# The opening of a two-layer trunk kernel: the first chunk's P1 and P2 moved ahead of the pair's eight steps

## The chip, the core and the metric

The kernel runs on one core of one Trainium2 chip. The core has five engines that run side by side and meet at semaphores: TensorE (matmuls; PE in the profile, its weight loads PEld), VectorE (DVE), ScalarE (ACT), GpSimd (POOL) and SyncE (SP, which here only issues transfers). Matmuls write into PSUM, which has eight banks of 128 x 512 fp32; everything else lies in SBUF, in tiles of 128 partitions. The metric is device microseconds of one execution, median of several runs. Each engine works through its own list of instructions in order, and each instruction starts when the tiles that it reads are written and the buffer that it writes is free.

## The reference

A trunk of two layers over 512 positions of width 1024, in fp32. Each layer has a SwiGLU block, a mixer and a second SwiGLU block, each after an RMSNorm, each added to the stream. The first layer's mixer is a gated linear recurrence, the second's a causal spatial gate.

```python
def swiglu(x, w_in, w_out):
    g, u = jnp.split(x @ w_in, 2, axis=-1)
    return (jax.nn.silu(g) * u) @ w_out
...
    for i in range(DEPTH):
        h = h + 0.5 * swiglu(rms_norm(h, ffn1_norm[i]), ffn1_w_in[i], ffn1_w_out[i])
        hn = rms_norm(h, mix_norm[i])
...
        h = h + m
        h = h + 0.5 * swiglu(rms_norm(h, ffn2_norm[i]), ffn2_w_in[i], ffn2_w_out[i])
    return rms_norm(h, final_norm)
```

The change touches only the start of the very first SwiGLU block: x (512 x 1024) times w_in (1024 x 5632), with the norm's gain on x's columns and its root on the result's rows.

## The kernel before

**One product.** An fp32 product is made of three matmuls: each operand is split into a high part, rounded to the format that TensorE reads (ScalarE copies it, `act` in L96), and a low part, the rest (VectorE subtracts, `tt` in L87 for weights, `stt` in L93 for x). The three are high by high, low by high and high by low. For x the blocks are turned by TensorE first (L267, a matmul with the identity), and the split reads the turned block out of PSUM with the norm's gain as its scale.

**Seven products instead of eight.** Large multiplications run through `seven` (L338): both operands are cut in 2 x 2 blocks and multiplied by a Strassen-Winograd scheme. Its seven products are P1 (A11), P2 (A12), P5 (S1), P6 (S2), P3 (S4), P7 (S3) and Q4 (A22), in this order, where A11 to A22 are quarters of the left operand and S1 to S4 sums of them (L46, L47). P1 and P6, P7, Q4 share the accumulators A, P2 has B, P5 and P3 have C (L48); each accumulator is two banks, one for each 128 rows. A stays open from P1 to Q4. Each product takes two steps, for its two halves of the inner dimension.

**Steps.** The program is a list of steps, `subs`. A step has a weight block of 128 x 1024 fp32 (`raw`, eight buffers), which it splits into `whi` and `wlo` (four buffers each), and twelve matmuls of 128 x 512. The main loop (L1457 to L1473) writes the program step by step: what is hooked to the step's phases "pre", "mid", "rest", the splits of the steps up to three ahead (`ahead`, L213, for the first ones), new loads as far as buffers are free (`load_more`), then the step's matmuls, then what is hooked to "end" and "late". So the place of every instruction in its engine's list is fixed here. A split that finds all four buffers taken waits for the matmuls of the step that used the oldest.

**Banks.** Of the eight banks six serve products (`bank`, L74) and two serve transposes and small things (`aux`, L77). A bank that the program asks for is one that an earlier tile has left, and the first matmul into it waits for that tile's last reader.

**The opening.** The first SwiGLU's columns are worked through as a pair (256 columns of gate and of value together, `pair_plain`, L736) and then chunks of four times 128. The pair isn't a `seven`: it multiplies A12, A11 (the first 256 rows: half 0), A22, A21 (the other rows: half 1) by its four weight blocks, each of which serves both halves, so the second half's four steps are `Again` and hold the split buffers of the first four until then. In steps 0 to 7 the pair runs; steps 8 and 9 are the chunk's P1, 10 and 11 P2, 12 and 13 P5, and so on. Because x's inverse root is not known yet, the pair's results wait for it: silu of half 0 in step 7, `post(0)` in step 8 (`stt` out of the banks p into h, L775), `post(1)` in step 9. The chunk's B takes its banks from `aux` here (`spare`).

**Loads.** SP issues loads in the order of the program: x's right half of the first 256 rows in two transfers of 256 columns, the first pair block in four transfers, the second in two, then x's left half, two more pair blocks (two transfers each), the other rows of x, and blocks as buffers come free. A pair block has rows of 1 KB (256 columns), or is cut further; a chunk's block has rows of 2 KB. Some blocks get a second block added by an accumulating transfer that GpSimd issues (`add`, L136), two steps after their load.

**The start of TensorE.** Before x arrives, TensorE runs matmuls on a tile of zeros (`warm_up`, L1381). Then A12's first block is turned, two more warm-ups, A12's second block, two more; the blocks are split together with the first weight blocks (L1423 to L1430). A11 is turned in the middle of step 1, A22 at the end of step 2, A21 at the end of step 3. `value` (L1412) copies a turned block unsplit, for the sums.

## Time and profile before

| | |
|---|---|
| median of 3 runs | 1618.13 us |
| lowest and highest | 1617.69, 1618.21 us |
| the profiled execution's own time | 1618.02 us |
| its span in the profile | 1616.1 us |
| granted TensorE clock | 0.999 |
| read from HBM | 275.84 MB, 172 GB/s over the span |

The profile is of one execution. The page's share of an engine is busy time over the span. Matmuls overlap in the pipeline: a matmul of 128 x 512 is shown with 0.39 us, and the next one starts 0.23 us after it. In a view by time a row merges like instructions of one line: start, time from the first's start to the last's end, engine, line, operation, tiles, count, and in brackets how long the engine was idle before it and what ended that. The page names the tiles by the program's names: `e` is a turned block, `hi` and `lo` its split, `whi` and `wlo` a weight block's, `raw` the block itself, `p`, `A`, `B`, `C` the accumulators, `h` the gated result.

### The profile page before, as it was taken

What the parts mean: (1) busy time and instruction counts of PE and PEld (TensorE: products, weight loads), DVE (VectorE), ACT (ScalarE), POOL (GpSimd) and SP (SyncE); (2) the same over time, 40 slices, a digit from 0 to 9 for tenths busy, and PEclk for the clock granted to TensorE, in tenths of its full rate; (3) what the DMA queues carried; (4) which work ended last, traced back from release to release, by engine and by line L of the source; (5) the groups of instructions that cost most, each with busy time, mean ns of one, the idle gap of its engine ahead of it and who ended that gap; (6) DMA issues with size and microseconds to landing.
All of it is one profiled execution on the core that took longest, in us unless ns stands there. A gap on an engine that the chain in (4) does not pass through costs nothing.

```text
span 1616.1 us, 20846 instructions
## 1 busy us (share of the span) xinstructions
PE 1604.8 (99%) x7451; PEld 1327.6 (82%) x7451; DVE 1373.2 (85%) x1839; ACT 1036.9 (64%) x1504; POOL 223.0 (14%) x201
## 2 busy tenths in 40 slices
PE   9999999999999999999999999999999999999998
PEld 7888888898888888888888888888888788888886
DVE  6898888888998787877987978878978988879778
ACT  7656556668776556656775565566886766565665
POOL 2111111100011111111101111111211011111110
PEclk9999999999999999999999999999999999999999
DMA  8767876844383786866837768768877557686693
GB/s 279 180 171 169 209 181 156 216 124 115 87 213 83 187 215 150 215 164 161 207 88 182 173 171 212 179 155 204 219 189 189 155 125 188 170 207 159 162 206 99
DMA packets 164695, 279.29 MB, mean 173 GB/s; under 512 B 11520, under 2 KB 38000, under 8 KB 164592
## 3 DMA queue, kind: packets, MB, share of 16 engines
q1 hardware_dynamic: 115088, 184.84, 36.4%
q0 software_dynamic: 47712, 91.30, 33.6%
q10 hardware_dynamic: 1792, 1.84, 0.4%
q8 instruction: 58, 0.95, 0.2%
q14 instruction: 45, 0.37, 0.1%
HBM read 275.84 MB, written 2.10 MB: 172 GB/s over the span
## 4 chain that ended last, share of the span: by engine, by line
PE 98%; ACT 1%; DMA 1%; DVE 0%; SPq 0%; issue 0%; DVEq 0%; ACTq 0%
PE A L367 14%; PE A L369 14%; PE A L368 14%; PE C L367 8%; PE C L368 8%; PE C L369 8%; PE p L760 5%; PE B L367 4%; PE B L369 4%; PE B L368 4%; PE e L267 4%; PE r L227 2%; PE r L225 2%; PE r L226 2%; PE Q L367 1%; PE Q L369 1%
## 5 line engine op out<-in xcount | busy, mean ns | idle before, releaser
L96 ACT ACTIVATE whi<-raw 128x1024 fp32r<-128x1024 f32 (+1 forms) x536 | 553.8, 1034 | 379.4 <-PE A L368 100.6
L87 DVE TENSOR_TENSOR wlo<-raw,whi 128x1024 fp32r<-128x1024 f32 (+1 forms) x537 | 638.6, 1191 | 182.2 <-ACT whi L96 180.8
L367 PE MATMUL A<-whi,hi 128*128 128x512 f32 x1016 | 403.9, 397 | 0.0
L369 PE MATMUL A<-wlo,hi 128*128 128x512 f32 x1016 | 396.7, 390 | 0.0
L368 PE MATMUL A<-whi,lo 128*128 128x512 f32 x1016 | 396.3, 390 | 0.0
L369 PEld LDWEIGHTS A<-wlo,hi 128*128 128x128 f32 x1016 | 190.7, 188 | 41.8 <-DVE wlo L87 0.3
L368 PEld LDWEIGHTS A<-whi,lo 128*128 128x128 f32 x1016 | 191.1, 188 | 38.0 <-DVE lo L87 0.6
L367 PEld LDWEIGHTS A<-whi,hi 128*128 128x128 f32 x1016 | 190.9, 188 | 37.4
L367 PE MATMUL C<-whi,hi 128*128 128x512 f32 x560 | 218.4, 390 | 0.0
L368 PE MATMUL C<-whi,lo 128*128 128x512 f32 x560 | 218.0, 389 | 0.0
L369 PE MATMUL C<-wlo,hi 128*128 128x512 f32 x560 | 217.9, 389 | 0.0
L137 POOL DMA_DIRECT2D raw<-in_ffn_w_in_dram x82 | 98.8, 1205 | 742.3 <-DVE raw L87 477.5
L137 POOL DMA_DIRECT2D raw<-in_ffn_w_out_dram x72 | 83.3, 1205 | 373.4 <-DVE wlo L87 158.9
L87 DVE TENSOR_TENSOR raw<-raw,raw 128x1024 f32<-128x1024 f32 x108 | 129.5, 1199 | 1.1 <-DMA raw<-in_ffn_w_out_dram 0.6
L87 DVE TENSOR_TENSOR lo<-a,hi 128x512 fp32r<-128x512 f32 (+1 forms) x188 | 122.2, 658 | 3.8 <-ACT hi L96 3.4
L96 ACT ACTIVATE hi<-a 128x512 fp32r<-128x512 f32 (+1 forms) x188 | 112.5, 601 | 20.2 <-DVE a L87 17.0
L368 PEld LDWEIGHTS C<-whi,lo 128*128 128x128 f32 x560 | 105.1, 188 | 22.1 <-DVE lo L87 0.2
L369 PEld LDWEIGHTS C<-wlo,hi 128*128 128x128 f32 x560 | 105.1, 188 | 21.8
L367 PEld LDWEIGHTS C<-whi,hi 128*128 128x128 f32 x560 | 105.1, 188 | 21.7
L96 ACT ACTIVATE c<-A 128x512 f32<-128x512 f32 x132 | 77.4, 594 | 54.9 <-PE A L369 54.9
L367 PE MATMUL B<-whi,hi 128*128 128x512 f32 x280 | 112.0, 400 | 0.0
L369 PE MATMUL B<-wlo,hi 128*128 128x512 f32 x280 | 109.3, 390 | 0.0
(161 smaller groups left out, 2103.7 us busy)
## 6 DMA issues: line engine op xcount, KB each, us to landing
raw<-in_ffn_w_in_dram SPq DMA_DIRECT2D x162, 512.0 KB, 4.4
raw<-in_ffn_w_out_dram SPq DMA_DIRECT2D x100, 512.0 KB, 5.6
raw<-in_ffn_w_in_dram POOLq DMA_DIRECT2D x82, 512.0 KB, 7.5
raw<-in_ffn_w_out_dram POOLq DMA_DIRECT2D x60, 512.0 KB, 7.6
raw<-in_sg_w_in_dram SPq DMA_DIRECT2D x20, 512.0 KB, 6.3
raw<-in_rec_w_in_dram SPq DMA_DIRECT2D x16, 512.0 KB, 4.0
raw<-in_ffn_w_in_dram SPq DMA_DIRECT2D x30, 256.0 KB, 5.1
raw<-in_sg_w_in_dram POOLq DMA_DIRECT2D x12, 512.0 KB, 8.1
```

Of the source, the lines that this page charges most:

```text
L87: nc.vector.tensor_tensor(out=o, in0=x, in1=y, op=op)
L96: nc.scalar.activation(out=o, in_=x, func=f, **k)
L137: nc.gpsimd.dma_start(out=self.v, in_=src, accum_op=ALU.add)
L225: nc.tensor.matmul(ps, wh, xh, start=start, stop=False)
L226: nc.tensor.matmul(ps, wh, xl, start=False, stop=False)
L227: nc.tensor.matmul(ps, wl, xh, start=False, stop=stop)
L267: nc.tensor.transpose(ps[:, o : o + P], src(q, s), ident)
L367: nc.tensor.matmul(ps, zh, wh, start=fresh and i == 0, stop=False, **k)
L368: nc.tensor.matmul(ps, zl, wh, start=False, stop=False, **k)
L369: nc.tensor.matmul(ps, zh, wl, start=False, stop=end, **k)
L760: nc.tensor.matmul(bank_of(half, s), z, (sub.lo if m == 2 else sub.hi)[:, q, :], start=left[2] == "2" and (h, q, m) == (0, 0, 0), stop=lef ...
```

## The change

P1 and P2 of the first chunk become steps 0 to 3, the pair steps 4 to 11; from step 12 on (P5) the order is as before. Therefore A11 is turned and split first and A12 in the middle of step 1 (`second_blocks`, now on banks of the products), A22 and A21 at the ends of steps 4 and 6 instead of 2 and 3. The first weight block is now the chunk's, loaded in two transfers of 2 KB rows, and x's first half comes in one transfer of 2 KB rows; A11's first block is split by quarters, the high part of the first by VectorE. P1's matmuls alternate between its two banks. The pair's matmuls have one order in all cases. `post(0)` stands in step 11, `post(1)` in step 13, the root in step 8, and the silu of c1 nine steps after P2. B's banks come from `bank`. The warm-ups are 6 and 2 instead of 5, 2 and 2.

```diff
         def fetch(self):
-            nc.sync.dma_start(out=self.v, in_=self.src)
+            for q in ((slice(0, 1), slice(1, 2)) if self.halves else (slice(0, self.shape[1]),)):
+                nc.sync.dma_start(out=self.v[:, q, :], in_=self.src[:, q, :])
...
-        def split(self, vector=False):
+        def split(self, between=None):
...
-                if vector:
-                    nc.vector.tensor_copy(self.hi[:, q, :], src[:, q, :])
-                else:
-                    act(self.hi[:, q, :], src[:, q, :], AF.Copy)
+                act(self.hi[:, q, :], src[:, q, :], AF.Copy)
                 tt(self.lo[:, q, :], src[:, q, :], f32(self.hi[:, q, :]), ALU.subtract)
+                if between is not None and q.start == 0:
+                    between()
...
-    ahead = {0: 1, 1: 1, 2: 3, 3: 3, 4: 3}
+    ahead = {0: 1, 1: 2, 2: 3, 3: 4, 4: 6, 5: 7}
...
-                        bk[name, s] = (spare if name == "B" else bank)(name)[:, :w]
+                        bk[name, s] = bank(name)[:, :w]
...
+                if opening and prod == "P1":
+                    qs = list(enumerate(pairs))
+                    for n, (q, i, m, s) in enumerate([(q, i, m, s) for q, i in qs for m in range(3) for s in range(2)]
+                                                     if ci == 0 else
+                                                     [(q, i, m, s) for m in range(3) for q, i in qs for s in range(2)]):
+                        if ci and n == 4:
+                            opening[0]()
+                        nc.tensor.matmul(bk[name, s], left(prod, i, s)[m == 1], (sub.lo if m == 2 else sub.hi)[:, q, :],
+                                         start=(i, m) == (0, 0), stop=(i, m) == (cuts[-1][-1], 2))
...
         for prod, ci in order:
+            if opening and (prod, ci) == ("P5", 0):
+                opening[1]()
...
-            hook(now[0] + 1, "mid", lambda: act(c1[s], c1[s], AF.Silu, scale=rt(s)))
+            hook(now[0] + (9 if opening else 1), "mid", lambda: act(c1[s], c1[s], AF.Silu, scale=rt(s)))
...
-            left_blocks(group, ht, half, 7 if first else 2)
+            left_blocks(group, ht, half, 4 - half if first else 2)
...
-                    end = (lambda: (hook(at0 + 7, "rest", lambda: (silu(0, 0), silu(0, 1))),
-                                    hook(at0 + 8, "mid", lambda: post(0)))) if first else lambda: post(0)
+                    end = (lambda: (hook(at0 + 6, "rest", lambda: (silu(0, 0), silu(0, 1))),
+                                    hook(at0 + 7, "mid", lambda: post(0)))) if first else lambda: post(0)
...
     raws[0].halves = True
-    load_x(0, 512, 256)
-    load_x(0, 768, 256)
+    load_x(0, 0)
     load_more(2)
-    load_x(0, 0)
-    load_more(4)
+    load_x(0, 512)
+    load_more(6)
     load_x(2, 512)
...
-    warm_up(5, 512)
+    warm_up(6, 512)
...
+    def part(i, name, q, vector=False):
+
+        g, c, gain = first.g[i], slice(q * H, (q + 1) * H), first.src(i, name)[1][q]
+        if name not in g.hl:
+            g.hl[name] = slot(F32R, "hi"), slot(F32R, "lo")
+        hi, lo = (t[:, c] for t in g.hl[name])
+        src = opening[i, name][:, c]
+        if vector:
+            ts(hi, src, gain, None, ALU.mult)
+        else:
+            act(hi, src, AF.Copy, scale=gain)
+        stt(lo, src, gain, f32(hi), ALU.mult, ALU.subtract)
...
+    def second_blocks():
+        turn(0, "A12", bank)
+        turn(1, "A12", bank)
+        parts(0, "A12")
+        parts(1, "A12")
+        subs[3].split()
+
+    turn(0, "A11")
+    turn(1, "A11")
     warm_up(2, 512)
...
+    part(0, "A11", 0, True)
+    subs[0].split(lambda: part(0, "A11", 1))
+    parts(1, "A11")
     subs[1].split()
...
+                         (2, "pre", lambda: (value(0, "A11", True), value(1, "A11", True))),
+                         (2, "rest", lambda: (value(0, "A12"), value(1, "A12"))),
+                         (4, "end", lambda: (turn(0, "A22"), turn(1, "A22"))),
+                         (5, "mid", lambda: (parts(0, "A22"), parts(1, "A22"))),
+                         (5, "rest", lambda: (value(0, "A22"), value(1, "A22", True))),
+                         (6, "end", lambda: (turn(0, "A21"), turn(1, "A21"))),
+                         (7, "mid", lambda: (parts(0, "A21"), parts(1, "A21"))),
+                         (7, "rest", lambda: (value(0, "A21"), value(1, "A21")))):
...
-    squares(6, "rest", "A21")
-    rstd(6, (0, "rest"), (0, "rest"), (1, "pre"))
-    first.rest(1, None)
+    squares(7, "rest", "A21")
+    rstd(8, (0, "pre"), (0, "pre"), (0, "rest"))
+    first.rest(4, None)
```

More of the change, by code (lines that the diff above doesn't have):

```diff
@@ L336, in left_of, with seven @@
         return left
-    def seven(block, cuts, left, w, posts, order=None, own=False, apart=False, joined=None, spare=bank):
+    def seven(block, cuts, left, w, posts, order=None, own=False, apart=False, joined=None, opening=None):
         bk, raw, held = {}, {}, []
@@ L355, in mm @@
                     for s in range(2):
-                        bk[name, s] = (spare if name == "B" else bank)(name)[:, :w]
+                        bk[name, s] = bank(name)[:, :w]
                 if prod == joined and ci == 0:
                     held.extend((sub, q, i) for q, i in enumerate(pairs))
+                    return
+                if opening and prod == "P1":
[7 more added lines that the diff above has]
+                                         start=(i, m) == (0, 0), stop=(i, m) == (cuts[-1][-1], 2))
+                    for s in range(2 * ci):
+                        posts[prod](s, bk[name, s])
                     return
@@ L685, in x_left, with chunk @@
         return left_of(lambda: S.z)
-    def chunk(w_in, f0, nt, group, first=False):
+    def chunk(w_in, f0, nt, group, opening=None):
         w = nt * P
@@ L733, in chunk @@
         seven(in_block(w_in, lambda n: n * DFF + f0 * P, w), [[0, 1], [2, 3]], x_left(), w,
-              dict(P1=p1, P2=p2, P5=p5, P6=p6, P3=p3, P7=p7, Q4=q4), own=first, spare=aux if first else bank)
+              dict(P1=p1, P2=p2, P5=p5, P6=p6, P3=p3, P7=p7, Q4=q4), own=bool(opening), opening=opening)
     def pair_plain(w_in, f0, group, first=False):
@@ L749, in bank_of, with product @@
             return st[half, s]
-        def product(sub, half, left, h, between=None):
-            sq = [(s, q) for q in range(2) for s in range(2)]
-            for i, (s, q, m) in enumerate([(s, q, m) for m in range(3) for s, q in sq] if first and h else
-                                          [(s, q, m) for q in range(2) for m in range(3) for s in range(2)] if first else
-                                          [(s, q, m) for s, q in sorted(sq) for m in range(3)]):
-                if i == 8 and between is not None:
-                    between()
+        def product(sub, half, left, h):
+            for s, q, m in [(s, q, m) for s in range(2) for q in range(2) for m in range(3)]:
                 z = S.z[h].hl[left][m == 1][:, q * H + s * P : q * H + (s + 1) * P]
@@ L782, in mm @@
                 def mm(sub, half=half, left=left, h=h):
-                    product(sub, half, left, h, opening["A11"] if first and (left, h) == ("A12", 1) else None)
+                    product(sub, half, left, h)
                 end = None
                 if (left, h) == ("A11", 1):
-                    end = (lambda: (hook(at0 + 7, "rest", lambda: (silu(0, 0), silu(0, 1))),
-                                    hook(at0 + 8, "mid", lambda: post(0)))) if first else lambda: post(0)
+                    end = (lambda: (hook(at0 + 6, "rest", lambda: (silu(0, 0), silu(0, 1))),
+                                    hook(at0 + 7, "mid", lambda: post(0)))) if first else lambda: post(0)
                 elif (left, h) == ("A21", 1):
@@ L800, in fetch @@
         def fetch(self):
-            for q in ((slice(0, 1), slice(1, 2)) if self.halves else (slice(0, 2),)):
-                for b, base in enumerate((0, DFF)):
-                    c0 = base + self.f0 * P
-                    ws = self.w_in[self.r0 + q.start * P : self.r0 + q.stop * P, c0 : c0 + 256]
-                    nc.sync.dma_start(out=self.v[:, q, b * 256 : (b + 1) * 256],
-                                      in_=ws.rearrange("(k p) c -> p k c", p=P))
+            for b, base in enumerate((0, DFF)):
+                c0 = base + self.f0 * P
+                ws = self.w_in[self.r0 : self.r0 + 2 * P, c0 : c0 + 256]
+                nc.sync.dma_start(out=self.v[:, :, b * 256 : (b + 1) * 256], in_=ws.rearrange("(k p) c -> p k c", p=P))
     def ffn(w_in, w_out, norm):
@@ L810, in ffn @@
         for i, sizes in enumerate(FF_PARTS):
-            groups, p0 = [], f0
+            groups, p0, pair, first = [], f0, None, not subs
             for n in sizes:
@@ L814, in ffn @@
                     groups.append(Group(1))
-                    pair_plain(w_in, f0, groups[-1], not subs)
+                    pair = lambda g=groups[-1], f0=f0: pair_plain(w_in, f0, g, first)
+                    if not first:
+                        pair()
                     f0 += 2
@@ L818, in ffn @@
                     groups.append(Group(n // 2))
-                    chunk(w_in, f0, n, groups[-1], len(subs) == 8)
+                    chunk(w_in, f0, n, groups[-1], (opening["A12"], pair) if first else None)
                     f0 += n
@@ L1332, in lru_consts @@
         yield
+    opening = {"A12": lambda: second_blocks()}
     last = FinalNorm()
@@ L1365, in load_more @@
             loaded += 1
-    opening = {}
     raws[0].halves = True
-    load_x(0, 512, 256)
-    load_x(0, 768, 256)
+    load_x(0, 0)
     load_more(2)
-    load_x(0, 0)
-    load_more(4)
+    load_x(0, 512)
+    load_more(6)
     load_x(2, 512)
@@ L1421, in value @@
             ts(t[:, c], ps[:, c], gain, None, ALU.mult)
-    turn(0, "A12")
-    warm_up(2, 512)
-    turn(1, "A12")
-    warm_up(2, 512)
-    parts(0, "A12")
-    subs[0].split()
-    parts(1, "A12")
+    def second_blocks():
[6 more added lines that the diff above has]
+    turn(1, "A11")
+    warm_up(2, 512)
+    part(0, "A11", 0, True)
+    subs[0].split(lambda: part(0, "A11", 1))
+    parts(1, "A11")
     subs[1].split()
-    value(0, "A12")
-    value(1, "A12")
-    opening["A11"] = lambda: (turn(0, "A11"), turn(1, "A11"))
     for n, phase, fn in ((0, "late", vec_rest),
-                         (2, "pre", lambda: (subs[2].split(True), parts(0, "A11"), parts(1, "A11"))),
-                         (2, "pre", lambda: (subs[3].split(), value(0, "A11", True), value(1, "A11", True))),
-                         (2, "end", lambda: (turn(0, "A22", bank), turn(1, "A22", bank))),
-                         (3, "pre", lambda: (parts(0, "A22"), parts(1, "A22"))),
-                         (3, "mid", lambda: (value(0, "A22"), value(1, "A22", True))),
-                         (3, "end", lambda: (turn(0, "A21"), turn(1, "A21"))),
-                         (4, "mid", lambda: (parts(0, "A21"), parts(1, "A21"))),
-                         (4, "rest", lambda: (value(0, "A21"), value(1, "A21")))):
+                         (2, "pre", lambda: (value(0, "A11", True), value(1, "A11", True))),
[6 more added lines that the diff above has]
+                         (7, "rest", lambda: (value(0, "A21"), value(1, "A21")))):
         hook(n, phase, fn)
```

## The prediction

> **What bounds the kernel now.** I read the page's busy shares and the chain of waits first, then busy time by stretch, then the opening in order of time.

> ```profile
> span 1616.1 us, 20846 instructions
> PE 1604.8 (99%) x7451; PEld 1327.6 (82%) x7451; DVE 1373.2 (85%) x1839; ACT 1036.9 (64%) x1504; POOL 223.0 (14%) x201
> PE 98%; ACT 1%; DMA 1%; DVE 0%; SPq 0%; issue 0%; DVEq 0%; ACTq 0%
> ...
> 200.00:1616.00 1416.00, 1407.56 (x6554) 1167.13 (x6552) 1203.88 (x1569) 909.52 (x1310) 187.25 (x161) 1.00 0.70 169
> 1600.00:1616.00 16.00, 8.23 (x37) 6.48 (x35) 11.16 (x29) 7.62 (x20) 0.00 (x0) 0.91 0.36 131
> ```

> TensorE is the bound, and after 200 us it is idle for 8.4 us, of which 7.8 us are the last 16. The change leaves that stretch alone, so all it can win lies in the opening, and whatever wait it adds on TensorE has no slack to vanish in.

> ```profile
> 1.26 2.32 PE L1384 MATMUL warm<-warm 128*128 128x512 bf16 x5 [1.26 <-DVE warm L1379]
> 3.90 1.11 PE L267 MATMUL e<-ident,x 128*128 128x128 f32 x4
> 5.62 0.60 PE L267 MATMUL e<-ident,x 128*128 128x128 f32 x4
> 6.59 1.27 ACT L96 ACTIVATE whi<-raw 128x512 fp32r<-128x512 f32 x2 [0.69 <-DMA raw<-in_ffn_w_in_dram]
> 7.27 0.73 PE L760 MATMUL p<-whi,hi 128*128 128x512 f32 x2 [0.62 <-ACT whi L96]
> 9.95 1.06 ACT L96 ACTIVATE whi<-raw 128x1024 fp32r<-128x1024 f32 x1 [1.36 <-DMA raw<-in_ffn_w_in_dram]
> 11.06 1.20 PE L760 MATMUL p<-whi,hi 128*128 128x512 f32 x4 [0.77 <-ACT whi L96]
> 12.88 0.69 DVE L184 CAST whi<-raw 128x1024 fp32r<-128x1024 f32 x1 [0.61 <-DMA raw<-in_ffn_w_in_dram]
> 13.03 1.04 PE L267 MATMUL e<-ident,x 128*128 128x128 f32 x8
> ...
> 33.07 0.39 PE L367 MATMUL A<-whi,hi 128*128 128x512 f32 x1
> ...
> 43.95 0.39 PE L367 MATMUL C<-whi,hi 128*128 128x512 f32 x1
> ```

> Columns: start, duration, engine and line, operation, idle time before and what ended it. From 33.07 to 43.95 stand 48 products: 0.2267 us each, so a step of twelve takes **2.72 us**. Eight transposes take 0.87 us of TensorE's time (13.03 to the next product at 13.9). The first product starts at 7.27, when the first weight block has landed and is rounded; the second step waits until 11.06 for the second block (landed 9.93, rounded 9.95 to 11.01). The first product of P5, at **43.95**, is my milestone: twelve steps lie before it in both kernels (eight of the pair, four of P1 and P2), with 24 transposes between their products. 144 x 0.2267 + 3 x 0.87 = 35.25 us, from 7.27 makes 42.5; the other 1.4 us are the wait at 11.06 and small ones. After P5 the order of work is the same.

> **The opening, new order.** Ahead of the second step stand the same bytes as before: half of x's first rows, block 0, block 1 (0.52 MB each), only in four transfers of 2 KB rows instead of eight of 1 KB rows. What counts is how fast they arrive.

> ```profile
> L1357 SPq DMA_DIRECT2D x<-in_x_dram x1: 435/435/435, 0.8 to 0.8; - x1
> DMA to landing us min/median/max: 3.0/3.0/3.0
> ...
> 4.72 0.47 SPq L1357 DMA_DIRECT2D x<-in_x_dram  x1
> ...
> 1.00:2.00 1.00, 0.74 (x2) 0.28 (x3) 0.20 (x1) 0.54 (x1) 0.76 (x3) 1.00 0.02 6
> 5.00:10.00 5.00, 4.38 (x21) 2.93 (x18) 3.09 (x6) 2.88 (x7) 1.19 (x3) 1.00 0.94 296
> 15.00:20.00 5.00, 5.00 (x27) 4.02 (x27) 4.90 (x12) 2.75 (x6) 0.00 (x0) 1.00 1.05 408
> ...
> 8.00:9.00 1.00, 1.00 (x7) 0.78 (x5) 0.97 (x2) 0.59 (x2) 0.00 (x0) 1.00 0.87 270
> ```

> The first rows are x's first quarter MB, issued at 0.81 and landed 3.0 us later, and the issue of x's second half; in the stretches the last two columns are DMA share and GB/s. Ends: (a) the bytes arrive by the old curve; (b) at the later 408 GB/s from 2.0 on, when data starts to flow. x's first 0.26 MB would take 0.64 us at that rate and landed at 3.8, so 1.2 us go to the slowest engine; block 1 is then there by 2.0 + 1.57 / 0.408 + 1.2 = 7.1. At (a) block 0's first half lands at 6.5, its ScalarE rounding takes 0.63 (half of 1.27), the first product starts at 7.2; block 1 is rounded at 11.0, 1.1 us after step 0 ends; P2's second product waits another 0.65. Milestone wanted at 7.2 + 35.25 + 1.1 + 0.65 = 44.2, a loss of 0.3. At (b) the x half lands at 4.5, eight transposes and two warm-ups end at 6.0, nothing waits but 0.1 in P2: 41.35, a gain of 2.6. That is the whole gain that can be had. x's second half has rows of 2 KB and was queued at 4.72, yet the rate at 8 to 9 us is still 270, so row size is not all of it, and I take a third of the way from (a) to (b): first product 6.75, block 1 landed 9.0, step 1 waits 0.65, P2 waits 0.6; 6.75 + 35.25 + 1.25 = 43.25, **gain 0.7 us**. [...]

> P2's wait comes from the queues: in step 1 the split of block 2 stands ahead of A12's rounding, on ScalarE (1.06) and on VectorE. Block 2 landed in time for 12.88 before; in the new order I put it at 11.8. Then 1.06 on ScalarE, 1.14 for its low part, 0.41 for A12's first low part:

> ```profile
> 28.89 0.62 ACT L96 ACTIVATE junk<-x 128x512 f32<-128x512 f32 x1
> 50.88 1.34 ACT L96 ACTIVATE c<-c,rt 128x512 f32<-128x512 f32 x2 [0.68 <-DVE c L87]
> ...
> 17.45 1.65 DVE L90 TENSOR_SCALAR a<-e,vec 128x256 f32<-128x256 f32 x4
> 21.94 1.57 ACT L96 ACTIVATE hi<-e,vec 128x256 fp32r<-128x256 f32 x4 [0.99 <-PE e L267]
> 22.81 1.66 DVE L93 SCALAR_TENSOR_TENSOR lo<-e,vec,hi 128x256 fp32r<-128x256 f32 x4 [1.17 <-ACT hi L96]
> ```

> 11.8 + 1.06 + 1.14 + 0.41, with hand-overs, is 14.5, and P2's second product was wanted at 13.9. Step 4 is next in line: VectorE still has block 3's low part (1.14), A11's four copies (1.65) and block 4's low part, which ends 20.1; the third product of step 4 wants it at 20.2. It just holds.

> Edits at zero: the new order inside the pair's steps (twelve products of one shape either way), one warm-up less (TensorE waits for x then anyway; 0.4 if not), the vector copy of block 2 that goes back to ScalarE (0.69 on one engine for 1.06 on the other, counted above), the squares and the root (two squares of 0.62 on ScalarE in a step of 2.72), c1's two silus nine steps later (P3 in step 16 needs them; cover gone, 0.67 each, half of 1.34), the pair's transposes for the second multiplication (steps 15 to 17 as before). SP issues seven transfers for the two halves of x and blocks 0 to 3 instead of thirteen, 0.47 us each, and the pair's blocks come four later; they are needed four steps later too, 11 us against 2.1 MB. P2's banks now come from the six of the products: two of these held only warm-ups by then, so zero; were it those of A12's transposes, P2 would wait until A12's copies end at 17.8, 4.1 us.

> **The new wait, at P5.** Six banks serve the products. Before, A was taken in step 8, after the pair's first half; now A holds two from step 0 through Q4, the pair's halves hold two each from steps 4 and 8, so all six are taken when P5 in step 12 asks for C's two. The only ones that come free are those of the pair's first half, after its last read, two multiplications on VectorE in step 11 ("mid", behind the low part of S2). In the old order these ran at 39.30, before C's 43.95. What VectorE must do first, by the old rows for the same instructions:

> ```profile
> 31.45 1.28 ACT L96 ACT_TABLE_LOAD   x1
> ...
> 39.30 0.87 DVE L93 SCALAR_TENSOR_TENSOR h<-p,rt,s 128x256 f32<-128x256 f32 x2
> ...
> 41.83 0.68 DVE L87 TENSOR_TENSOR lo<-a,hi 128x512 fp32r<-128x512 f32 x1
> ...
> 43.21 0.68 DVE L93 SCALAR_TENSOR_TENSOR s<-a,a 128x512 f32<-128x512 f32 x1
> 43.81 1.22 DVE L87 TENSOR_TENSOR raw<-raw,raw 128x1024 f32<-128x1024 f32 x1
> 44.95 1.22 DVE L87 TENSOR_TENSOR wlo<-raw,whi 128x1024 fp32r<-128x1024 f32 x1
> 46.08 0.69 DVE L87 TENSOR_TENSOR lo<-a,hi 128x512 fp32r<-128x512 f32 x1
> ...
> 61.29 1.06 ACT L96 ACTIVATE whi<-raw 128x1024 fp32r<-128x1024 f32 x1 [0.68 <-PE C L368]
> ```

> By the starts, 1.14 us for a 1024-wide instruction and 0.60 for a 512-wide one. The last row shows a split that waits for TensorE to leave a buffer: the four split buffers hold the pair's blocks until steps 8 to 11 have used them a second time, so P5's first split cannot begin before step 8 ends. Count from there: 0.2 hand-over, 1.06 on ScalarE; on VectorE the low parts of blocks 12, 13, 14 and the sums into blocks 14 and 15 (5 x 1.14 = 5.7), low parts of S1, S2, S2 and the sums S2 and S4 (5 x 0.60 = 3.0), the first multiplication 0.44: 10.4 to 10.7 with hand-overs. TensorE reaches P5 three steps later, 8.16. So P5 waits **2.5 us** (2.2 to 2.6), whatever the opening did. ScalarE is not later: the table load (1.28) and two silus in step 10 are done 2 us before the multiplication. Behind the waiting product stands all of TensorE. VectorE catches up meanwhile and no later step shows a new want.

> Sum: -0.7 + 2.5 = **+1.8 us**. The profiled execution took 1618.02, 1.9 around its span of 1616.1; that makes 1619.8, and on the median of 1618.13, 0.1 higher, 1619.9. Own range from 2.2 - 1.5 to 2.6 + 0.1: 1618.8 to 1620.8. A difference of 0.2%, 3.2 us, is about what can be told from none here.

> **Rivals.**

> 1. Not slower: the transfers reach the full 408 GB/s. Then -2.6 + 2.5 = -0.1, 1618.0; were the wait at P5 half as long too, 1616.8. It decides from block 1 landing by 7.3. For it: four transfers ahead instead of eight; against it the 270 GB/s at 8 us.
> 2. The opening loses, and the sums into the raw blocks come late. Old curve +0.3, P5 +2.5 makes 1620.9. The accumulating transfers on POOL's queue may add to it:

> ```profile
> 26.53 1.21 POOL L137 DMA_DIRECT2D raw<-in_ffn_w_in_dram  x1 [1.34 <-DMA raw<-in_ffn_w_in_dram]
> raw<-in_ffn_w_in_dram POOLq DMA_DIRECT2D x4, 512.0 KB, 8.6
> ...
> 41.07 1.10 ACT L96 ACTIVATE whi<-raw 128x1024 fp32r<-128x1024 f32 x1
> ```

>    Block 13's, issued at 26.5, lands 8.6 later, near 35; ScalarE split that block at 41.07 and now wants it at 38.0. With later loads brought forward against it, 5.5 us late would put VectorE 1.5 back: 1622.4.
> 3. TensorE runs at its slow rate for longer. The first five warm-ups took 2.32 us, 0.43 each against 0.2267 later, and the first four transposes 1.11 against 0.60 for the next. The granted clock says 1.00 all the while, so only durations show it. Now TensorE stands idle between the warm-ups (1.26 + 6 x 0.43 = 3.8) and x at 4.9; and P5's 2.5 us would be the longest pause of the kernel. At half rate for 4 us, as long as the opening shows, it loses 2 us at either place: 1619.9 + 2.0 = 1621.9, both 1623.9. Against it: the 0.77 us at 11.06 left the rate as it was. [...]

> **How the numbers follow.** Forecast 0.52; rival 1 0.10; rival 2 0.15; rival 3 0.20; P2 on the wrong banks 0.03 (1624). Slower by over 0.2% is above 1621.4: a third of rival 2, nearly all of rival 3, the banks, and 0.04 of the forecast: 0.31. Faster by over 0.2%, below 1614.9, needs more than the whole gain of the opening: 0.02. Within: 0.67. The range goes past the forecast's own on both sides, over rival 1's -0.1 and all of rival 2, and leaves out the far end of rival 1 (0.03), the banks and the upper part of rival 3 (0.1): 1617.6 to 1622.4.

> **What would show it.** The first product of P1 near 6.8, with an idle row on ScalarE's rounding; block 1 landing near 9; a VectorE-released wait of 0.6 in P2; P5's first product ready near 43.2 but released near 45.7 by the multiplication that writes h; about 1.8 us more from the milestone on. No such wait at P5, or one let go by ScalarE or a transfer, breaks the forecast; products 0.43 apart near 7 us or after P5 mean rival 3.

## The result and the profile after

| | before | after |
|---|---|---|
| median of 15 runs | 1618.21 us | 1621.67 us |
| lowest and highest | 1617.50, 1619.76 | 1619.24, 1622.11 |
| ratio of after to before | | 1.0019, 95% interval 1.0012 to 1.0026 |
| the profiled execution's own time | 1618.02 | 1621.86 |
| its span | 1616.1 | 1619.9 |

The change costs 3.5 us by the medians and 3.8 us by the spans. The forecast of 1619.9 had the sign; it lies 1.8 us below the median, which is inside the stated range (1617.6 to 1622.4) but above the forecast's own (1618.8 to 1620.8).

The page of the changed kernel, its span, its busy times and the row of the products into C:

```profile
span 1619.9 us, 20843 instructions
PE 1606.9 (99%) x7450; PEld 1329.8 (82%) x7450; DVE 1372.6 (85%) x1839; ACT 1037.9 (64%) x1504; POOL 221.9 (14%) x201
L381 PE MATMUL C<-whi,hi 128*128 128x512 f32 x560 | 219.0, 391 | 2.6 <-DVE h L93 2.6
```

The last two columns of the third row are idle time ahead of the group and what ended most of it: 2.6 us, ended by VectorE's write of h. TensorE's busy time has grown too, by 2.1 us over before, although it has the same products. The first growth is a wait; the second means that some products took longer.

TensorE around P5, in order of time, first before and after the wait:

```profile
43.69 0.39 PE L770 MATMUL p<-wlo,hi 128*128 128x512 f32 x1
46.63 0.52 PE L381 MATMUL C<-whi,hi 128*128 128x512 f32 x1 [2.55 <-DVE h L93]
46.95 0.63 PE L382 MATMUL C<-whi,lo 128*128 128x512 f32 x1
47.37 0.63 PE L383 MATMUL C<-wlo,hi 128*128 128x512 f32 x1
...
49.93 0.57 PE L383 MATMUL C<-wlo,hi 128*128 128x512 f32 x1
50.34 0.40 PE L381 MATMUL C<-whi,hi 128*128 128x512 f32 x1
```

and VectorE in the same stretch:

```profile
43.13 1.22 DVE L87 TENSOR_TENSOR raw<-raw,raw 128x1024 f32<-128x1024 f32 x1
44.27 1.21 DVE L87 TENSOR_TENSOR wlo<-raw,whi 128x1024 fp32r<-128x1024 f32 x1
45.40 0.68 DVE L87 TENSOR_TENSOR lo<-a,hi 128x512 fp32r<-128x512 f32 x1
46.00 0.87 DVE L93 SCALAR_TENSOR_TENSOR h<-p,rt,s 128x256 f32<-128x256 f32 x2
```

P5 was ready to start at 43.69 + 0.23 = 43.92 and started at 46.63: **2.7 us**, let go by the multiplication that empties the pair's banks, which stands behind a sum, a split and a low part on VectorE. Then products start 0.43 us apart instead of 0.23, up to 50.34. The granted clock in those stretches (busy time and count of each engine; then granted clock, DMA share, GB/s):

```profile
43.90:46.75 2.85, 0.30 (x2) 0.15 (x2) 2.85 (x5) 2.29 (x4) 0.97 (x1) 1.00 0.00 0
46.75:47.00 0.25, 0.25 (x2) 0.19 (x3) 0.25 (x2) 0.25 (x1) 0.23 (x1) 0.81 0.00 0
47.00:50.25 3.25, 3.25 (x9) 2.57 (x8) 2.81 (x4) 0.26 (x1) 1.19 (x1) 0.50 0.83 122
50.25:50.50 0.25, 0.25 (x2) 0.17 (x2) 0.00 (x0) 0.00 (x0) 0.00 (x0) 0.86 1.25 229
```

The clock is halved right after TensorE has begun again, and comes back at 50.3. The shares 0.81 and 0.86 place the two edges: 47.00 - 0.38 x 0.25 = 46.905 and 50.25 + 0.28 x 0.25 = 50.32, so half rate for some 3.4 us. (The packed trace keeps the clock as records with start and length, of which the views show averages; its record of the half clock starts at 46.905 and lasts 3.413.) At half rate 3.4 us do the work of 1.7: **1.7 us** are lost behind the wait.

The opening of the changed kernel, TensorE and ScalarE by time:

```profile
1.26 2.74 PE L1393 MATMUL warm<-warm 128*128 128x512 bf16 x6 [1.26 <-DVE warm L1388]
...
5.15 1.97 PE L267 MATMUL e<-ident,x 128*128 128x128 f32 x8 [0.94 <-DMA x<-in_x_dram]
...
7.41 1.42 PE L369 MATMUL A<-whi,hi 128*128 128x512 f32 x2
8.63 0.96 PE L369 MATMUL A<-whi,lo 128*128 128x512 f32 x2
...
9.01 1.06 ACT L96 ACTIVATE whi<-raw 128x1024 fp32r<-128x1024 f32 x1
...
9.43 0.63 PE L369 MATMUL A<-wlo,hi 128*128 128x512 f32 x2
...
11.52 1.06 ACT L96 ACTIVATE whi<-raw 128x1024 fp32r<-128x1024 f32 x1 [1.44 <-DMA raw<-in_ffn_w_in_dram]
```

Eight transposes take 1.97 us from the first's start to the last's end, where eight took 1.04 at full rate before (at 13.03), and the products are 0.4 us apart or more until 9.4. Block 1 landed at 8.83 and is rounded from 9.01, near the forecast, but TensorE, still in step 0, doesn't wait for it. So the head start is spent: P5 is wanted at 43.92, against 43.95 before. The views show the granted clock as 1.00 here, but they can't tell: the trace's first record of the clock starts at 9.358, at full rate, and a view counts the time ahead of it as full:

```profile
5.10:7.40 2.30, 2.25 (x10) 1.91 (x11) 1.06 (x3) 0.63 (x1) 1.09 (x3) 1.00 1.00 352
7.40:9.40 2.00, 2.00 (x6) 1.61 (x5) 1.92 (x4) 1.99 (x5) 0.00 (x0) 1.00 1.06 396
```

The two rows also show the transfers: 352 and 396 GB/s; the whole stretch from 5 to 10 us has 376, and had 296 before. Sum: 0.0 + 2.7 + 1.7 = 4.4 us at P5; summed over the matmul starts, some 0.3 of that comes back between 50 and 100 us, and the spans differ by 3.8. The last 0.3 lies behind the start of the last matmul, from which the span runs on for 8.3 us before and 8.0 after.

### The profile page after: what moved, and what is told of

Its sections match the earlier page's. It is cut to its first block, busy times and chain, and to the rows that moved or that the text cites. A ratio compares the mean times of both kernels' runs of the same rounds, so it can differ in the third digit from the quotient of the medians.

```text
span 1619.9 us, 20843 instructions
## 1 busy us (share of the span) xinstructions
PE 1606.9 (99%) x7450; PEld 1329.8 (82%) x7450; DVE 1372.6 (85%) x1839; ACT 1037.9 (64%) x1504; POOL 221.9 (14%) x201
## 4 chain that ended last, share of the span: by engine, by line
PE 97%; DVE 1%; ACT 1%; DMA 0%; issue 0%; DVEq 0%
PE A L381 14%; PE A L383 14%; PE A L382 14%; PE C L381 8%; PE C L382 8%; PE C L383 8%; PE p L770 5%; PE B L381 4%; PE B L383 4%; PE B L382 4%; PE e L267 4%; PE r L227 2%; PE r L225 2%; PE r L226 2%; PE Q L383 1%; PE Q L381 1%
## 5 line engine op out<-in xcount | busy, mean ns | idle before, releaser
L96 ACT ACTIVATE whi<-raw 128x1024 fp32r<-128x1024 f32 (+1 forms) x537 | 554.9, 1034 | 385.1 <-PE A L382 100.7
L87 DVE TENSOR_TENSOR wlo<-raw,whi 128x1024 fp32r<-128x1024 f32 (+1 forms) x537 | 638.6, 1191 | 185.9 <-ACT whi L96 184.9
L87 DVE TENSOR_TENSOR raw<-raw,raw 128x1024 f32<-128x1024 f32 x108 | 129.4, 1198 | 1.1 <-DMA raw<-in_ffn_w_out_dram 0.6
L96 ACT ACTIVATE hi<-a 128x512 fp32r<-128x512 f32 (+1 forms) x188 | 112.4, 601 | 20.2 <-DVE a L87 17.0
L87 DVE TENSOR_TENSOR lo<-a,hi 128x512 fp32r<-128x512 f32 (+1 forms) x188 | 122.0, 656 | 3.8 <-ACT hi L96 3.4
L96 ACT ACTIVATE c<-A 128x512 f32<-128x512 f32 x132 | 77.4, 594 | 56.1 <-PE A L383 56.1
## 6 DMA issues: line engine op xcount, KB each, us to landing
raw<-in_ffn_w_in_dram SPq DMA_DIRECT2D x161, 512.0 KB, 4.5
raw<-in_ffn_w_out_dram SPq DMA_DIRECT2D x100, 512.0 KB, 5.3
raw<-in_ffn_w_in_dram POOLq DMA_DIRECT2D x82, 512.0 KB, 7.3
raw<-in_ffn_w_out_dram POOLq DMA_DIRECT2D x60, 512.0 KB, 7.9
raw<-in_sg_w_in_dram SPq DMA_DIRECT2D x20, 512.0 KB, 6.1
raw<-in_rec_w_in_dram SPq DMA_DIRECT2D x16, 512.0 KB, 3.8
raw<-in_sg_w_in_dram POOLq DMA_DIRECT2D x12, 512.0 KB, 8.2
```

Source lines behind the costliest of these rows:

```text
L87: nc.vector.tensor_tensor(out=o, in0=x, in1=y, op=op)
L96: nc.scalar.activation(out=o, in_=x, func=f, **k)
```

## The experiments

The theory after this reading: (1) the pause at P5 is the banks' wait alone, and (2) the pause makes TensorE lose its rate, a second price; (3) the opening's gain is real but is lost when TensorE stays at its slow rate until 9 us. The rivals: the pause hides another wait that appears once the banks are free; the slow products come from something else (the loads that start again at 47); the opening gains nothing because the loads are slow. All ratios below are to the kernel before, measured in the same sessions.

**Other banks for the pair's second half.** The second half takes the two spare banks, and A21's transposes take banks of the products instead.

```diff
-                st[half, s] = bank("p")
+                st[half, s] = (aux if first and half else bank)("p")
...
-                         (6, "end", lambda: (turn(0, "A21"), turn(1, "A21"))),
+                         (6, "end", lambda: (turn(0, "A21", bank), turn(1, "A21", bank))),
```

> The pair's second half takes its two banks from the two auxiliary ones (and A21 is turned into banks of the products), so that C finds two free banks at P5. Theory (C waits for the banks of the pair's first half, and TensorE's rate halves after that pause): no wait of 2.7 us before C's first product, no products 0.43 us apart behind it, together 4.4 us less than the changed kernel, 1617.3 to 1617.9 us, a little under the kernel before. Rival (VectorE is simply behind at P5, the bank only shows it): C waits for another VectorE result, the low parts of S1 or of the weights, and most of the 4.4 us stays, above 1620. Rival (the cost is the opening's): 1621.7 stays.

Measured: **1616.65** (1616.33 to 1617.74), ratio 0.9992 (0.9983 to 1.0001), 5.0 us below the changed kernel and 0.7 below the lower end of what was expected. In its trace C follows p without a gap, while VectorE reaches the multiplication as late as in the changed kernel:

```profile
43.90 0.39 PE L770 MATMUL p<-wlo,hi 128*128 128x512 f32 x1
44.13 0.39 PE L381 MATMUL C<-whi,hi 128*128 128x512 f32 x1
...
46.21 0.87 DVE L93 SCALAR_TENSOR_TENSOR h<-p,rt,s 128x256 f32<-128x256 f32 x2
```

So VectorE's queue was not late for anything but these banks, and no other wait stood behind them. The profiled execution is the slowest of its eleven (1617.74) and has the slow opening: its eight transposes take 1.97 us, and pairs of products start 0.86 us apart at 8.65, against 0.47 from 10.10 on.

**The pause filled.** Ten matmuls on the zero tile, in a spare bank, at the end of step 11. The wait stays, TensorE is busy in it.

```diff
+    def fill(n):
+        ps = aux("fill")
+        for _ in range(n):
+            nc.tensor.matmul(ps, warm[:, :P], warm, start=True, stop=True)
+
+    hook(11, "end", lambda: fill(10))
```

> The changed kernel with ten matmuls on the zero tile (2.3 us of TensorE's time at the full rate) ahead of C's first product, in the pause. Theory (the slow products behind the pause, 8 of them 0.2 us too long, come from the pause itself): the pause is filled, C's first product still starts 2.7 us late, but the products behind it stand 0.227 us apart: 1.7 us less, 1620.0 us. Rival (C's first products are slow for another reason, such as their weights or the load on VectorE): 0.43 us apart as in the changed kernel, 1621.7 us.

Measured: **1619.89** (1618.46 to 1621.83), ratio 1.0010 (1.0001 to 1.0019), 1.8 below the changed kernel. The trace:

```profile
42.20 0.39 PE L770 MATMUL p<-wlo,hi 128*128 128x512 f32 x1
42.44 2.33 PE L1472 MATMUL fill<-warm 128*128 128x512 bf16 x10
45.14 0.47 PE L381 MATMUL C<-whi,hi 128*128 128x512 f32 x1 [0.38 <-DVE h L93]
45.45 0.39 PE L382 MATMUL C<-whi,lo 128*128 128x512 f32 x1
45.68 0.40 PE L383 MATMUL C<-wlo,hi 128*128 128x512 f32 x1
```

P5 starts as late after its last p, which started at 42.20, as in the changed kernel (45.14 - 42.20 = 2.94; 46.63 - 43.69 = 2.94), and the products behind it run at full rate. Behind the filled pause the granted clock is 1.00 from 45.1 to 48.5, with 99 GB/s of transfers, against 0.54 from 46.6 to 50.3 with 111 GB/s in the changed kernel: here the slow products came with TensorE's idleness, not with the transfers or the wait.

**Eight warm-ups instead of six.** It fills the gap between 4.0 and x's arrival.

```diff
-    warm_up(6, 512)
+    warm_up(8, 512)
```

> The changed kernel with 8 warm-ups ahead of the first transposes instead of 6, so that TensorE is busy until 4.7 us and not until 3.8. Theory (the pause of 1 us ahead of x keeps the slow rate until 9 us, where the kernel before reached the full rate near 5.6): transposes 0.11 us apart, first product of P1 near 6.8 instead of 7.4, products 0.23 us apart from the first on, second step near 10.1 instead of 11.25, 0.8 to 0.9 us less, 1620.8 us. Rival (the rate changes at a fixed time or by itself): transposes still 0.21 us apart and slow products until 9 us, 1621.7 us.

Measured: **1620.14** (1619.03 to 1621.15), ratio 1.0009 (1.0000 to 1.0018), 1.5 below the changed kernel, where 0.8 to 0.9 was expected. Its trace has the fast opening and then the pause and the slow products:

```profile
1.26 3.57 PE L1393 MATMUL warm<-warm 128*128 128x512 bf16 x8 [1.26 <-DVE warm L1388]
...
5.19 1.09 PE L267 MATMUL e<-ident,x 128*128 128x128 f32 x8 [0.19 <-DMA x<-in_x_dram]
...
6.51 0.70 PE L369 MATMUL A<-whi,hi 128*128 128x512 f32 x2
...
45.81 0.77 PE L381 MATMUL C<-whi,hi 128*128 128x512 f32 x1 [2.53 <-DVE h L93]
46.38 0.63 PE L382 MATMUL C<-whi,lo 128*128 128x512 f32 x1
```

**The multiplication first in step 11.** `post(0)` ahead of everything else of the step, the change's own banks, six warm-ups.

```diff
-                                    hook(at0 + 7, "mid", lambda: post(0)))) if first else lambda: post(0)
+                                    hook(at0 + 7, "pre", lambda: post(0)))) if first else lambda: post(0)
```

> The changed kernel with the two multiplications that free C's banks ahead of the sum into block 15 and the split of block 14 in step 11, instead of behind them and S2's low part: three places up VectorE's list, 2.9 us. Theory: they run near 43.1 instead of 46.0, C's first product starts within 0.2 us of step 11's end at 43.9 and at the full rate, 4.2 us less, 1617.5 us; what is put back by 0.8 us (the split of block 14) has 5 us to spare. Rival (VectorE is the bound of this stretch): P6 in step 14 waits for block 14 or S2 instead, 1619 us or more.

Measured: **1616.91** (1615.85 to 1617.59), ratio 0.9991 (0.9983 to 1.0000): 0.6 below what was expected; no pause, and nothing waits for the instructions that moved behind it. Its profiled execution is the fastest of all here (1615.85) and has the fast opening with six warm-ups; those of the filled pause above and of the shorter pause below have it too. Its order up to there is the changed kernel's, its rate is not:

```profile
1.26 2.74 PE L1393 MATMUL warm<-warm 128*128 128x512 bf16 x6 [1.26 <-DVE warm L1388]
3.94 0.27 PE L1398 MATMUL vec<-ident,first_gain 8*128 8x8 f32 x1
5.06 1.10 PE L267 MATMUL e<-ident,x 128*128 128x128 f32 x8 [0.85 <-DMA x<-in_x_dram]
...
42.49 0.40 PE L381 MATMUL C<-whi,hi 128*128 128x512 f32 x1
```

So the opening's rate differs between executions when the gap is there: the eight transposes took 1.10 us here behind 0.85 us of idle time, and 1.97 us in the changed kernel's trace behind 0.94.

**Both cures: other banks and eight warm-ups.** The edits of the first and the third experiment.

```diff
-                st[half, s] = bank("p")
+                st[half, s] = (aux if first and half else bank)("p")
...
-    warm_up(6, 512)
+    warm_up(8, 512)
```

> The pair's second half on the auxiliary banks (as in the first run) and 8 warm-ups ahead of x instead of 6. Theory (the two losses, the pause at P5 with its slow products and the slow rate in the opening, are separate and add; with 8 warm-ups most executions have the full rate when x comes): 0.7 us less than with the banks alone, 1615.9 us, and a narrower spread. Rival (the rate at 5 us hangs on the moment at which the execution starts, whatever TensorE does then): 1616.6 us, the same spread as with the banks alone.

Measured: **1616.22** (1615.97 to 1616.78), ratio 0.9989 (0.9980 to 0.9997), the narrowest spread of all. It is 0.4 below the banks alone, where 0.7 was expected, and the interval of its ratio lies below 1: this version beats both kernels. Its opening and its P5:

```profile
5.20 1.09 PE L267 MATMUL e<-ident,x 128*128 128x128 f32 x8 [0.50 <-DMA x<-in_x_dram]
6.53 0.70 PE L369 MATMUL A<-whi,hi 128*128 128x512 f32 x2
...
9.94 1.20 PE L369 MATMUL A<-whi,hi 128*128 128x512 f32 x4 [0.25 <-ACT whi L96]
...
43.16 0.39 PE L381 MATMUL C<-whi,hi 128*128 128x512 f32 x1
```

P5 starts at 43.16, 0.8 ahead of before. Between the opening of the first run (slow in its profiled execution, P5 at 44.13) and this one lies 1.0 us.

**x's first rows in two transfers.** The other banks again, x in two transfers of 1 KB rows as before the change, five warm-ups and two after each pair of transposes.

```diff
-    load_x(0, 0)
+    load_x(0, 0, 256)
+    load_x(0, 256, 256)
...
-    warm_up(6, 512)
+    warm_up(5, 512)
...
+    warm_up(2, 512)
```

> The banks as in the first run, but x's first half in two transfers of 256 columns and the warm-ups as in the kernel before (5, then 2 behind each block of transposes). Measures what the 2 KB rows of x are worth. Theory (fewer, longer rows are why block 1 landed at 8.8 instead of 9.9): block 1 lands some 0.3 later, near 9.1; the first transposes start at 3.9 instead of 5.15 and TensorE has no pause, so the full rate is there by 5.7; first product near 6.8; 1616.3 us, between the banks alone and the banks with 8 warm-ups. Rival (x's transfer does not matter, the order of the steps does): block 1 at 8.8 as with one transfer, 1615.9 us.

Measured: **1616.49** (1616.08 to 1618.40), ratio 0.9990 (0.9981 to 0.9999). Block 1 is rounded as soon as in the kernel with both cures, which has one transfer (8.82); block 2 later (11.48 there):

```profile
8.76 1.06 ACT L96 ACTIVATE whi<-raw 128x1024 fp32r<-128x1024 f32 x1 [0.39 <-DMA raw<-in_ffn_w_in_dram]
11.90 1.06 ACT L96 ACTIVATE whi<-raw 128x1024 fp32r<-128x1024 f32 x1 [2.08 <-DMA raw<-in_ffn_w_in_dram]
```

Block 1's rounding started at 8.76 here, at 8.47, 8.82 and 9.01 in three traces with x in one transfer (multiplication first, both cures, the change), and at 9.95 before the change. So the form of x's transfer is not what brought block 1 forward. That leaves the weight blocks' own rows (three transfers of 2 KB rows instead of six of 1 KB rows or less ahead of the second step), which were not tried by themselves.

**A shorter pause.** `post(0)` one place up, ahead of S2's low part.

```diff
-                                    hook(at0 + 7, "mid", lambda: post(0)))) if first else lambda: post(0)
+                                    hooks.setdefault((at0 + 7, "mid"), []).insert(0, lambda: post(0)))) if first else lambda: post(0)
```

> The changed kernel with the two multiplications that free C's banks one place up VectorE's list, ahead of S2's low part alone: 0.6 us earlier, so the pause at P5 is 2.1 us instead of 2.7. Theory (the rate is lost when the pause is long against a window of the clock's): products behind the pause mostly at the full rate, 0.6 + about 1 us less, 1620.0 us. Rival (any pause of some 2 us costs the same slow stretch): only the 0.6 us are saved, 1621.1 us.

Measured: **1620.40** (1618.57 to 1622.12), ratio 1.0013 (1.0005 to 1.0022). The median is between the two; the trace decides for the rival in that execution. The pause is 2.1 us (45.16 - 42.81 - 0.23) and the clock is halved for as long as behind the longer one:

```profile
42.81 0.39 PE L770 MATMUL p<-wlo,hi 128*128 128x512 f32 x1
45.16 0.56 PE L381 MATMUL C<-whi,hi 128*128 128x512 f32 x1 [1.95 <-DVE h L93]
45.52 0.63 PE L382 MATMUL C<-whi,lo 128*128 128x512 f32 x1
```

```profile
45.25:45.50 0.25, 0.25 (x1) 0.17 (x2) 0.25 (x2) 0.25 (x1) 0.25 (x1) 0.79 0.00 0
45.50:48.75 3.25, 3.25 (x9) 2.56 (x8) 3.25 (x5) 0.90 (x2) 1.32 (x2) 0.50 0.59 66
48.75:49.00 0.25, 0.25 (x2) 0.20 (x2) 0.20 (x1) 0.00 (x0) 0.25 (x1) 0.88 1.07 197
```

That a pause counts against a window of the clock's was the author's conjecture, which no run shows; what this run shows is 1.95 us of idle time and 3.4 us at a clock of 0.50 behind it.

**Shorter still, with eight warm-ups.** `post(0)` two places up, ahead of block 14's low part as well.

```diff
-                                    hook(at0 + 7, "mid", lambda: post(0)))) if first else lambda: post(0)
+                                    hook(at0 + 7, "add", lambda: post(0)))) if first else lambda: post(0)
...
-    warm_up(6, 512)
+    warm_up(8, 512)
...
                 subs[q + 1].add()
+                run("add")
```

> Eight warm-ups ahead of x, banks as in the change, and post(0) two places up in step 11, ahead of block 14's low part as well. The pause at P5 should fall from 2.7 to about 1.0 us (0.60 for S2's low part and 1.14 for block 14's taken out of the wait). The kernel with the same eight warm-ups and no pause took 1616.22. If a pause of 1 us keeps TensorE's rate, this takes 1616.2 + 1.0 = 1617.2 and the products behind the pause start 0.23 us apart; if any pause loses it, eight or nine products stand 0.43 apart behind it and the time is near 1618.9.

Measured: **1617.46** (1617.14 to 1618.14), ratio 0.9995 (0.9986 to 1.0004). The pause is there, with 0.81 us of idle time, and the rate is kept, at a granted clock of 1.00 from 43.90 to 47.30:

```profile
42.70 0.39 PE L770 MATMUL p<-wlo,hi 128*128 128x512 f32 x1
43.89 0.47 PE L381 MATMUL C<-whi,hi 128*128 128x512 f32 x1 [0.81 <-DVE h L93]
44.20 0.40 PE L382 MATMUL C<-whi,lo 128*128 128x512 f32 x1
44.43 0.40 PE L383 MATMUL C<-wlo,hi 128*128 128x512 f32 x1
```

A pause of 1.0 us cost 1.0 us; by the medians 1.1 to 1.2 over the two kernels without it, below and above. One of 2.1 or 2.7 us that TensorE spent idle cost 1.6 to 1.7 us on top in each of the three executions that were profiled.

**The multiplication first, with eight warm-ups.** The fourth and the third experiment together, on the change's own banks.

> Eight warm-ups ahead of x and post(0) at the very start of step 11, with the change's own banks. No pause at P5. If the time depends on the pause and on the opening's rate alone, it equals the kernel with the second half's banks from the spare pair and eight warm-ups, 1616.22, within 0.5, and spreads as little (about 1 us). If the earlier multiplication holds VectorE up where something waits for it, it is later by up to 0.9, the two multiplications' time: 1617.1. With six warm-ups this place took 1616.91.

Measured: **1616.36** (1616.02 to 1616.90), ratio 0.9987 (0.9978 to 0.9996). In its trace C follows p without a gap:

```profile
43.10 0.40 PE L381 MATMUL C<-whi,hi 128*128 128x512 f32 x1
```

It equals the kernel with other banks: two cures of different kind, one of the bank and one of the order on VectorE, come to one time, and both beat the kernel before.

Side by side:

| pause at P5 | six warm-ups | eight warm-ups |
|---|---|---|
| 2.7 us | 1621.67 (the change) | 1620.14 |
| 2.1 us | 1620.40 | |
| 2.7 us, filled | 1619.89 | |
| 1.0 us | | 1617.46 |
| none, other banks | 1616.65 | 1616.22 |
| none, multiplication first | 1616.91 | 1616.36 |

## Why the prediction was right in sign and short in size

- **The wait at P5** was forecast at 2.5 us (2.2 to 2.6), released by the multiplication that writes h. It measured 2.7, a tenth past its range, on that releaser, with VectorE's instructions in the order counted. Right, and shown by taking the banks' want away (other banks) and by taking VectorE's lateness away (multiplication first): either removes all of it.
- **What the pause does to TensorE** is the failed step. Rival 3 had the mechanism, TensorE at its slow rate after P5, at 2 us and a chance of 0.20, and the prediction argued against it with the 0.77 us at 11.06, a pause a third as long. It measured 1.7 us, and it belongs in the sum, which put it at nothing. The half clock behind it lasted 3.413 us. That a pause of some 2.5 us leaves the rate as it was, as the sum had it, is what the traces refute: TensorE was idle for 2.55 of the 3.4 us before the drop in the changed kernel and for 1.95 in the kernel with the shorter pause. The forecast's own range, up to 1620.8, does not reach the median. The stated range does, because its upper end of 1622.4 was taken from rival 2, which did not happen; that the price of rival 3's mechanism stays below it is in part luck.
- **The opening's 0.7 us gain** exists, and was put a little low: in the seven traces where the change's opening ran fast, P5 is wanted at 42.4 to 43.2, 0.8 to 1.5 ahead of before; 43.25 was forecast. Of its parts, the first product starts at 6.4 to 6.7 there (6.75 forecast, 7.41 in the changed kernel's trace), and block 1 landed at 8.83 in the changed kernel (9.0 forecast); that the loads would come a third of the way between the two ends was the author's estimate. The rate from 5 to 10 us grew from 296 to 376 GB/s; which edit did that was not separated. In the profiled execution of the changed kernel the gain was spent on the slow rate until 9.4, rival 3's other half: P5 wanted at 43.92. That the granted clock is 1.00 all the while was a misreading: the clock has no record there (before the change the first one starts at 5.558), and the durations tell the rate.
- **P2's wait** of 0.6 for A12's low part is absent in the changed kernel, which reaches P2 late. Where the opening is fast it is there in part: 0.24 to 0.30 of idle time in three traces and 0.65 in the kernel with x in two transfers, at most 0.14 in the other four. It was a fair term for the forecast's opening, at its upper end.
- **The zeros** held: with the pause gone, the matmul starts show in one later stretch of 50 us alone a loss of more than 0.2 us against the kernel before (0.31 from 1100 to 1150 us, in the kernel with x in two transfers; the two with eight warm-ups and no pause gain 0.2 there). The late accumulating transfers of rival 2 did not happen, rival 1's full-rate loads neither, and P2's banks were free.

The forecast's terms with their measured sizes: opening -0.7 became 0.0, the wait +2.5 became +2.7, and +1.7 for the rate was missing; 0.3 came back between 50 and 100 us and 0.3 behind the last matmul, which makes the 3.8 by the spans.

What stays open: six warm-ups against eight differ by 1.5 us with the pause and by 0.4 to 0.6 without it. The traces show the slow opening and the slow products only for the profiled executions. The times hint that the loss behind the pause comes in some executions and not in others: with eight warm-ups and the pause, five of eleven runs took 1619.03 to 1619.38, about the pause above the kernel without it (1616.22), and six took 1620.14 to 1621.15; the profiled one, with the loss, is of the second group (1620.87). The granted clock points the same way, 0.998 and 0.999 in the first group, 0.997 and 0.998 in the second, but no execution of the first was traced. The kernels with a long pause spread over 2.1 to 3.6 us, the two with a cure and eight warm-ups over 0.8 and 0.9. Why the change's own runs are mostly at the upper end isn't known (one of fifteen took 1619.24, at a clock of 0.999).

## What to carry to other kernels

When a reordering holds accumulators open for longer, count the banks at every step and find the instruction that frees the last one; a wait there is cured either by a bank elsewhere or by moving that one instruction up its own engine's list, and here the two gave 5.0 and 4.8 us. Price a pause of TensorE at its length plus what the clock does after it: here, in the executions profiled, 1.0 us cost 1.0, and 2.7 cost 4.4. For a pause that can't be avoided, ten matmuls on a tile of zeros held the rate here (clock 1.00 behind it, 1.8 us off the changed kernel), and eight such matmuls ahead of the first data instead of six took 1.5 us off the time with the pause and 0.4 to 0.6 without it, and narrowed the spread of the kernels without it from 1.4 and 1.7 us to 0.8 and 0.9.

## What the runs showed of the hardware

One opening had two rates. With six warm-ups TensorE was idle for 0.85 to 0.98 us ahead of x. In three traces (filled, shorter pause, multiplication first) the eight transposes behind that gap took 1.09, 1.10 and 1.10 us; in the other two (the change, other banks) they took 1.97. The gap is as long in both groups, 0.94, 0.97 and 0.85 us against 0.94 and 0.98, so its length doesn't tell them apart; what does was not shown.

The loss did not need 3.4 us without work: 1.95 us idle in the 3.4 ahead of the drop was enough. In the kernel before, the 0.77 us ahead of 11.06 left the rate: the granted clock is 1.00 from 10 to 15 us. The pause with 0.81 idle left it too, and by the times none of its eleven runs lost 1.7 us (1617.14 to 1618.14). No pause with an idle time between 0.8 and 1.9 us was measured at P5.
